# Three GpSimd drains inside the tile loop of a hard-max attention kernel, at tiles 28, 60 and 92

## The chip, the cores and the metric

The kernel runs on one core of a Trainium2 chip. The metric is the device time of one execution in microseconds (us). The kernel before takes 466.72 us (median of 3 runs, 466.47 to 467.32). All engine names are those of the profile: PE is TensorE, PEld its weight loads, DVE is VectorE, ACT is ScalarE, POOL (or Pool) is GpSimd, SP is SyncE.

## The reference

For each of 4 × 4096 queries, find the key with the largest dot product and return its value row:

```python
def reference(q, k, v):                                # each [4, 4096, 128] float32
    logits = np.matmul(q, k.transpose(0, 2, 1))
    best = np.argmax(logits, axis=-1)
    b_idx = np.arange(q.shape[0])[:, None]
    return v[b_idx, best, :].astype(np.float32)
```

## The kernel before

The 16384 queries are cut into T = 128 tiles of 128 queries. PE, ACT and DVE screen all keys of a tile in fp16. What DVE keeps is an index of a group of three keys per query (`cand`). Pool then gathers those three keys from memory (`kg`), and DVE computes their products with the query again (`prod`, then adds). Two tiles form a pair: it has two k gathers and one product. When a chunk of 4 or 8 tiles is through, DVE picks the winners (`win`), and Pool gathers their value rows (`vr`), which SP stores.

So for each tile Pool issues one k gather and one v gather. With the loads of later batches and some gathers for doubtful rows, these are 324 DMAs in the whole program, all started by instructions on Pool. The last of them is a scatter into the output.

The gathers are appended to queues. `near_q` holds k gathers and, after the last gather of each pair, a *mark*; `late_q` holds v gathers:

```python
    def gather(c, t0, n):                      # a pair: tiles t0, t0 + 1
        ...                                    # cut: cand on DVE
        kg = rp.tile([P, n, 3, P], FP16, tag=f"kg{n}", name=f"kg_{t0}", bufs=8)
        kg_t[t0] = kg
        for j in range(n):
            near_q.append(lambda j=j: nc.gpsimd.indirect_dma_start(
                out=kg[:, j].rearrange("p f d -> p (f d)"), out_offset=None, in_=k16[t0 // NQT],
                in_offset=IOA(ap=x[:, j:j + 1], axis=0)))
        mark = lambda: done.add(("kg", t0))
        marks.add(mark)
        near_q.append(mark)
        start(dots(c, t0, n), "dots", c)

    def dots(c, x, m):
        ...
        yield "until", lambda: ("kg", x) in done, 1 if x >= TAIL else 2     # TAIL = T - 24
        kg = kg_t.pop(x)
        prod = rp.tile([P, m, 3, P], FP16, tag=f"prod{m}", name=f"prod_{x}")
        nc.vector.tensor_tensor(out=prod, in0=kg, in1=natq[...], op=OP.mult)     # cut
```

At the end of each tile, `issue` decides which gathers go out:

```python
    def issue(it):
        n = 0
        clock[0] = it
        put_out(it)
        while near_q and (n < 1 + (it >= T - 28 and len(near_q) > 2) or near_q[0] in marks):
            g = near_q.pop(0)
            n += g not in marks
            g()
        if fast and it >= rest[0]:
            fast.pop(0)()
            rest[0] = it + 3
        take_late(2 if n == 0 and len(late_q) > 4 or it >= T - 24 and it % 2 == 0 else 1)
```

The loop calls it once per tile:

```python
    for it in range(T):
        ...                                    # cut: loads, transposes
        if it > 0:
            screen(it)                         # PE, ACT
        if it >= 1:
            fold(it - 1)                       # DVE: W
        ...
        step(it)                               # one DVE instruction of the products and picks
        if it >= 2:
            top(it - 2)                        # DVE: TOP
        if 3 <= it <= TAIL:
            gathers(it - 3)                    # DVE: cand, fills near_q
        if it >= TAIL:
            gathers(it - 2)
        step(it)
        issue(it)                              # Pool
```

The trace shows one more instruction of weight, which the code above doesn't contain: the program ends with a drain on Pool.

## Time and profile before

| | before |
|---|---|
| time, median of 3 runs | 466.72 us |
| span of the profiled run | 465.5 us |
| DVE busy | 417.8 us (90%) |
| Pool busy | 318.1 us (68%) |
| last product starts at | 425.92 us |
| from there to the end | 39.6 us |
| sequencer instruction before the last scatter (trace) | 2.41 us |
| final Pool drain (trace) | 10.49 us, 454.19 to 464.68 |

The first lines below are from the page of the profile before: the span, each engine's busy time, and the groups of the k gathers, the v gathers and the products. A group's line gives source line, engine, operation, what is written and read, and count; then busy time and mean nanoseconds of one; then idle time of the engine just before them and what ended most of it.

```profile
span 465.5 us, 6396 instructions
PE 380.2 (82%) x1834; PEld 168.3 (36%) x1834; DVE 417.8 (90%) x825; ACT 376.8 (81%) x437; POOL 318.1 (68%) x345
...
L250 POOL DMA_INDIRECT kg<-k,cand x128 | 127.4, 995 | 85.1 <-issue 26.6
...
L304 POOL DMA_INDIRECT vr<-in_v_dram,win x128 | 136.6, 1067 | 39.0 <-issue 37.5
...
L265 DVE TENSOR_TENSOR prod<-kg,natq 128x768 f16<-128x768 f16 x64 | 34.9, 546 | 3.9 <-DMA kg<-k,cand 3.9
```

DVE is the engine that sets the pace. Its products wait only 3.9 us for k gathers in the whole run.

The end is Pool's. This is Pool's timeline before, in its last 20 us (start, duration, engine, line, operation; in brackets the idle time before it and what ended that):

```profile
447.55 1.00 POOL L498 DMA_INDIRECT FV<-in_v_dram,xw_fe  x1 [2.19 <-DVE hi L573]
454.42 1.03 POOL L534 DMA_INDIRECT out_dram<-FV,rowk_e  x1 [5.87 <-issue]
```

After the scatter at 454.42 nothing more is busy, yet the run goes on for 10 us: that is the drain. Drains don't count as busy and don't stand in the timeline. The trace has them with start and end, and the times of drains here are read from it. The Trainium skill, "Perfetto Trace Analysis", section "Sequencer-only Instruction (DRAIN, etc)", draws a drain as an instruction of the sequencer alone; this trace agrees, since the final drain's record opens at 454.19 and the scatter executes on Pool from 454.42 to 455.45, inside it. A drain's own work is therefore counted below from the end of the last DMA: 464.68 − 455.45 = 9.23 us.

The other thing that stands out is two DMAs that start late for no reason that a wait shows. They are the ones with index 113 and 219 (counted from 0) in Pool's order; no semaphore instruction stands before them on Pool. (The scatters at 287 and 323 also start late, but the trace shows semaphore instructions just before them.) First the lines around index 113 (the load, which here follows a gather with 0.135 us of gap where other loads have none), then those around 219 (gap 0.79 where gathers have 0.30):

```profile
164.65 1.01 POOL L304 DMA_INDIRECT vr<-in_v_dram,win  x1 [0.30 <-issue]
165.79 0.59 POOL L67 DMA_DIRECT2D natq<-in_q_dram  x1
...
303.90 0.99 POOL L304 DMA_INDIRECT vr<-in_v_dram,win  x1 [0.30 <-issue]
305.68 0.95 POOL L250 DMA_INDIRECT kg<-k,cand  x1 [0.79 <-issue]
```

### The profile page before, as it was taken

The numbers are of one execution on the slowest core, as the hardware profiler recorded it, in microseconds if no ns is written. First come the engines' busy times: TensorE is split into PE (matmuls) and PEld (weight loads), VectorE is DVE, ScalarE is ACT, GpSimd is POOL, SyncE is SP. The second block draws the span as 40 slices with busy tenths as digits, with TensorE's granted clock in tenths as the row PEclk, the third lists the DMA queues.
The fourth block names the chain that finished last, engine by engine and source line by source line (L and its number), as shares of the span: only waits on it lengthen the run. The fifth ranks groups of instructions, "written<-read, shape, count | busy, mean of one in ns | idle before, by whom it ended". The sixth has DMA issues, their size and how long they took to land.

```text
span 465.5 us, 6396 instructions
## 1 busy us (share of the span) xinstructions
PE 380.2 (82%) x1834; PEld 168.3 (36%) x1834; DVE 417.8 (90%) x825; ACT 376.8 (81%) x437; POOL 318.1 (68%) x345
## 2 busy tenths in 40 slices
PE   8999999998999889999998889998998888850100
PEld 4444444443444344444443334443333333320000
DVE  2689999999999999999999999999998999998330
ACT  2999999999999989999997889999998888840000
POOL 8233557877677888776678876677777777767730
PEclk9999999999999999999999999999999999995555
DMA  7934576853325877943235653423432333322320
GB/s 130 227 66 96 107 103 97 139 120 85 80 76 135 148 140 128 121 126 81 79 98 137 129 116 94 100 80 87 110 101 79 86 86 99 87 71 68 94 74 4
DMA packets 43624, 47.54 MB, mean 102 GB/s; under 512 B 25000, under 2 KB 33451, under 8 KB 43584
## 3 DMA queue, kind: packets, MB, share of 16 engines
q0 software_dynamic: 18752, 30.97, 33.7%
q1 hardware_dynamic: 24832, 16.13, 13.1%
q8 instruction: 14, 0.23, 0.2%
q14 instruction: 26, 0.21, 0.2%
HBM read 39.59 MB, written 12.19 MB: 111 GB/s over the span
## 4 chain that ended last, share of the span: by engine, by line
DVE 31%; issue 23%; ACT 13%; PE 13%; DMA 9%; POOL 7%; POOLq 0%; DVEq 0%; ACTq 0%
DVE W L228 14%; ACT A L202 10%; PE psn L193 5%; DVE TOP L232 5%; PE psn L212 4%; DMA kg<-k,cand 4%; ACT E L215 4%; DMA vr<-in_v_dram,win 3%; DVE prod L265 3%; PE pd L193 3%; POOL kg L250 3%; POOL vr L304 2%; DVE D L274 2%; DVE p L269 2%; DMA natk<-in_k_dram 2%
## 5 line engine op out<-in xcount | busy, mean ns | idle before, releaser
L202 ACT ACTIVATE A<-pd 128x1024 f16<-128x1024 f32 x256 | 258.6, 1041 | 23.0 <-PE pd L193 22.7
L250 POOL DMA_INDIRECT kg<-k,cand x128 | 127.4, 995 | 85.1 <-issue 26.6
L228 DVE SCALAR_TENSOR_TENSOR W<-psn,E 128x1024 int16<-128x1024 f32 x128 | 166.0, 1297 | 7.0 <-ACT E L215 5.5
L193 PE MATMUL pd<-kT,qT 128*128 128x512 f16 x512 | 151.8, 378 | 15.7 <-ACT A L202 14.8
L193 PE MATMUL psn<-kT,qT 128*128 128x512 f16 x512 | 151.8, 378 | 15.3 <-ACT A L202 7.9
L304 POOL DMA_INDIRECT vr<-in_v_dram,win x128 | 136.6, 1067 | 39.0 <-issue 37.5
L193 PEld LDWEIGHTS <-qT 128*128 128x128 f16 x1024 | 98.4, 97 | 163.9 <-issue 76.0
L232 DVE MAX8 TOP<-W 128x8 f32<-128x1024 f32 x128 | 155.8, 1217 | 0.0
L212 PE MATMUL psn<-A,identh 128*128 128x512 f16 x512 | 152.1, 378 | 0.0
L215 ACT ACTIVATE E<-psn 128x1024 int16<-128x1024 f32 x128 | 132.2, 1033 | 5.0 <-PE psn L212 5.0
L212 PEld LDWEIGHTS <-identh 128*128 128x128 f16 x512 | 49.6, 97 | 60.8
L265 DVE TENSOR_TENSOR prod<-kg,natq 128x768 f16<-128x768 f16 x64 | 34.9, 546 | 3.9 <-DMA kg<-k,cand 3.9
L269 DVE TENSOR_TENSOR p<-prod 128x384 f16<-128x384 f16 x64 | 22.3, 349 | 0.1
L274 DVE TENSOR_REDUCE D<-p 128x6 f32<-128x192 f16 x64 | 21.5, 336 | 0.1
L173 ACT ACTIVATE kT<-uk 128x256 f16<-128x256 f32 x48 | 20.1, 419 | 0.9 <-PE uk L170 0.9
L64 POOL DMA_DIRECT2D natk<-in_k_dram x27 | 16.1, 599 | 0.9 <-POOLq L795 0.8
L67 POOL DMA_DIRECT2D natq<-in_q_dram x27 | 16.3, 605 | 0.2
L169 PE MATMUL uk<-identh,natk 128*128 128x128 f16 x96 | 15.8, 218 | 0.6 <-ACT A L202 0.6
L272 DVE TENSOR_TENSOR p<-p 128x192 f16<-128x192 f16 x64 | 15.7, 245 | 0.0
L464 PE MATMUL fp_e<-n_e,tri 128*128 128x1 f32 x2 | 0.6, 361 | 16.7 <-DVE n_e L462 16.7
L170 PEld LDWEIGHTS <-natk 128*128 128x128 f16 x96 | 9.3, 97 | 7.7 <-issue 5.3
L169 PEld LDWEIGHTS <-natk 128*128 128x128 f16 x96 | 9.3, 97 | 5.6
(147 smaller groups left out, 133.5 us busy)
## 6 DMA issues: line engine op xcount, KB each, us to landing
out_dram<-vr SPq DMA_DIRECT2D x32, 256.0 KB, 2.2
natq<-in_q_dram POOLq DMA_DIRECT2D x26, 128.0 KB, 3.2
k<-kd SPq DMA_DIRECT2D x8, 384.0 KB, 4.2
natk<-in_k_dram POOLq DMA_DIRECT2D x24, 128.0 KB, 3.9
kg<-k,cand POOLq DMA_INDIRECT x128, 2.8
vr<-in_v_dram,win POOLq DMA_INDIRECT x128, 2.8
natq<-in_q_dram POOLq DMA_DIRECT2D x1, 768.0 KB
natk<-in_k_dram POOLq DMA_DIRECT2D x1, 512.0 KB, 5.2
```

What stands on the lines that cost most here:

```text
L169: nc.tensor.matmul(out=o, lhsT=natk[b % 2][:, h, 4 * m + x, :], rhs=identh, start=True, stop=False)
L193: nc.tensor.matmul(out=ps[:, n * 512:(n + 1) * 512], lhsT=qT[b % 2][:, qt * P:(qt + 1) * P], rhs=kT[b % 2][:, u * 1024 + n * 512:u * 1024 ...
L202: nc.scalar.activation(out=A, in_=ps, func=AF.Abs)
L212: nc.tensor.matmul(out=ps[:, n * 512:(n + 1) * 512], lhsT=identh, rhs=A[:, n * 512:(n + 1) * 512], start=False, stop=True)
L215: nc.scalar.activation(out=E, in_=ps, func=AF.Relu, scale=QSCALE)
L228: nc.vector.scalar_tensor_tensor(out=W_t[t % NW].bitcast(I16)[:, 1::2], in0=ps, scalar=QSCALE, in1=E, op0=OP.mult, op1=OP.max)
L232: nc.vector.max(out=TOP[:, t, :], in_=W_t[t % NW].bitcast(FP32))
L250: near_q.append(lambda j=j: nc.gpsimd.indirect_dma_start(out=kg[:, j].rearrange("p f d -> p (f d)"), out_offset=None, in_=k16[t0 // NQT], ...
L265: nc.vector.tensor_tensor(out=prod, in0=kg, in1=natq[b % 2][:, x - b * NQT:x - b * NQT + m, :].unsqueeze(2).to_broadcast([P, m, 3, P]), op ...
L269: nc.vector.tensor_tensor(out=p1, in0=prod[:, :, :, 0:64], in1=prod[:, :, :, 64:128], op=OP.add)
L274: nc.vector.tensor_reduce(out=d[:, x - c0:x - c0 + m, 1:4], in_=p2, axis=AX_X, op=OP.add)
L304: late_q.append(lambda j=j: nc.gpsimd.indirect_dma_start(out=vr[:, j, :], out_offset=None, in_=v_flat, in_offset=IOA(ap=win[:, i + j:i + j ...
```

## The change

The intent, as the change reads: the final drain has something to clear up for the DMAs that Pool issued. If Pool clears part of it earlier, in the loop, where DVE sets the pace and Pool has spare time, then less is left for the end, where Pool is alone. To make room, the three tiles with a drain issue no gathers; the k gather is made up soon after, the v gathers within some tiles.

```diff
+DRAINS = (28, 60, 92)
 ...
     def issue(it):
         n = 0
         clock[0] = it
         put_out(it)
-        while near_q and (n < 1 + (it >= T - 28 and len(near_q) > 2) or near_q[0] in marks):
+        if it in DRAINS:
+            nc.gpsimd.drain()
+            owed[0] += 2
+            return
+        behind = len(near_q) > (2 if it >= T - 28 else 4)
+        while near_q and (n < 1 + behind or near_q[0] in marks):
             g = near_q.pop(0)
             n += g not in marks
             g()
         if fast and it >= rest[0]:
             fast.pop(0)()
             rest[0] = it + 3
-        take_late(2 if n == 0 and len(late_q) > 4 or it >= T - 24 and it % 2 == 0 else 1)
+        more = n == 0 and len(late_q) > 4 or it >= T - 24 and it % 2 == 0
+        if owed[0] and n < 2 and it % 3 == 0 and len(late_q) > 2:
+            owed[0] -= 1
+            more = True
+        take_late(2 if more else 1)
+
+    owed = [0]
```

## The prediction

> **What bounds the kernel now.** The page gives VectorE (DVE) 417.8 of 465.5 us busy (90%); in a table of 20 us windows it is full nearly throughout from 40 to 420 us. A tile costs it 3.0 to 3.3 us (distance of W folds in its timeline). GpSimd (Pool, 68%) runs beside it: in its timeline a k gather takes 0.98 us, a v gather 1.01, each after a 0.30 us issue gap, so 2.6 us per tile; with a load (0.60) 3.2. A gather lands 2.8 us after issue (DMA issues); usually 3 to 5 us pass between a pair's landing and its product on DVE, but at pairs 46 and 48 below 1 us, at pair 104 none. After 426 us comes a serial tail of 40 us, all Pool at its end: a sequencer instruction of 2.41 us (450.8), the last scatter (454.4) and the final Pool drain, 10.49 us (454.19 to 464.68). The scatter, at the usual 2.8 us, lands at 457.2; about 7.5 us of the drain is something else.
>
> **What the drain does.** I suppose it retires one record for each Pool DMA on a list. The Trainium skill, "DMA: Bandwidth & Descriptors", section "SWDGE vs HWDGE vs iDMA", says that GpSimd keeps its descriptors in rings in SBUF.[...] Of 324 Pool DMAs, two start late with no wait that explains it: index 113 (gap 0.135 instead of 0.00) and index 219 (0.79 instead of 0.30). I read these as the ring filling, being freed in bulk, cheaply, and filling again 106 later. Then some 112 records are left for the final drain: 7.5/112 = 0.067 us each (estimate).
>
> **The change.** Removed: 2.6 us of Pool work in each of tiles 28, 60, 92. Added: three drains behind about 64, 79 and 73 DMAs, by the same estimate 4.3, 5.3 and 4.9 us (about 2 us, the last landing, if retiring is cheap). Moved: the k gather is made up two tiles later; two v gathers come 5 and 8 tiles later, one more than skipped, so about three of the 11 v gathers after 424 us leave the tail. Left for the final drain: about 109 DMAs, no fewer than the 112 above. So I expect the final drain to stay at 10 us and the 2.41 us instruction too: the saving that the change seems made for does not come. Fewer v gathers in the tail save about 0.6 us.
>
> **On the critical path.** Replaying the timeline's Pool issues with these drains against the products' start times, DVE stalls little at 28, 1 to 2 us around tile 60, and most after 92, where Pool is busy without a break until 345 us and pair 104 has no slack: in all +6 us with 0.067 us per record, +1.5 us if a drain only waits for landings.
>
> **Prediction.** 470 us (+0.7%), 459.5 to 477 in 8 of 10. Faster by over 2%: 0.05; within 2%: 0.83; slower by over 2%: 0.12.
>
> **What would show it.** Right: three Pool drains of 4 to 6 us; a final drain of still 9 to 11 us; odd gaps at indices 113 and 219 gone; products waiting for k gathers after tiles 60 and 92; DVE busy time unchanged.
>
> **What would make it wrong.** If the list holds all 324 DMAs (0.023 to 0.028 us each), the loop's drains take about 2 us, fit into the freed tile, and the final drain falls to about 4 us and the 2.41 to about 0.8: then some 460 us. If drains only wait for landings, 467.5. If drains are dearer than estimated, over 476.

## More of the kernel before

The `yield "until"` line decides where the product stands in DVE's program: two tiles after the pair's mark, and one tile after it for pairs from tile 104 on. This is settled when the program is built.

The busy time of each engine in windows, in this order: window, length, PE, PEld, DVE, ACT, POOL, granted clock, DMA share, GB/s:

```profile
195.00:225.00 30.00, 28.72 (x142) 12.80 (x140) 30.00 (x51) 29.07 (x36) 20.81 (x22) 1.00 0.38 98
300.00:330.00 30.00, 27.94 (x126) 11.92 (x125) 30.00 (x54) 28.56 (x33) 22.80 (x23) 1.00 0.32 83
360.00:400.00 40.00, 33.06 (x137) 13.05 (x136) 39.56 (x95) 31.63 (x34) 29.79 (x31) 1.00 0.31 87
```

In two 30 us windows of the loop DVE has no idle time at all.

## The result, and the profile after

The changed kernel takes 482.78 us (median of 4 runs, 480.9 to 483.78) where the kernel before took 466.67 in the same rounds. The ratio is 1.0338, with a 95% interval of 1.0301 to 1.0375: slower by 3.4%.

| | before | after |
|---|---|---|
| span of the profiled run | 465.5 us | 480.2 us |
| DVE busy | 417.8 us | 418.8 us |
| products waiting for k gathers | 3.9 us | 17.3 us |
| last product starts at | 425.92 us | 440.11 us |
| from there to the end | 39.6 us | 40.1 us |
| sequencer instruction before the last scatter | 2.41 us | 2.31 us |
| final Pool drain | 10.49 us | 10.06 us |

The lines of the page after that answer to those of before:

```profile
span 480.2 us, 6397 instructions
PE 383.3 (80%) x1834; PEld 168.5 (35%) x1834; DVE 418.8 (87%) x825; ACT 377.6 (79%) x437; POOL 316.4 (66%) x345
...
L251 POOL DMA_INDIRECT kg<-k,cand x128 | 128.4, 1003 | 98.6 <-issue 38.1
...
L305 POOL DMA_INDIRECT vr<-in_v_dram,win x128 | 134.3, 1049 | 39.0 <-issue 36.9
...
L266 DVE TENSOR_TENSOR prod<-kg,natq 128x768 f16<-128x768 f16 x64 | 35.3, 551 | 17.5 <-DMA kg<-k,cand 17.3
```

Nothing got more work to do: DVE's busy time is the same within 1 us. Its products wait 13.4 us longer. The same windows as before:

```profile
195.00:225.00 30.00, 27.59 (x135) 12.29 (x134) 29.25 (x50) 27.99 (x35) 17.45 (x19) 1.00 0.33 81
300.00:330.00 30.00, 27.64 (x127) 11.79 (x126) 27.11 (x50) 28.17 (x32) 17.92 (x18) 1.00 0.27 70
360.00:400.00 40.00, 30.72 (x121) 11.77 (x120) 35.93 (x95) 28.42 (x31) 29.20 (x30) 0.96 0.29 84
```

In the first two windows, which hold a drain each, Pool is busy 3.4 and 4.9 us less than before and DVE now has 0.8 and 2.9 us of idle time. In the third there is no drain (the last drain ended at 312.41), and DVE still loses 3.6 us against before. So a second cause seems to act late in the loop. The waits of DVE for k gathers split between the two stretches. These are the lines of the waits of after, first in the window from 95 to 366 us, then in that from 366 to 441 us, each with total, count and longest:

```profile
DVE prod L266 <- DMA kg<-k,cand: 8.6, 12, 2.5
...
DVE prod L266 <- DMA kg<-k,cand: 8.8, 4, 3.7
```

In the same two windows of before the totals were 2.9 and 1.0 us. (The windows are the same times, not the same tiles, in the two kernels.)

Pool's timeline of after shows what a drain costs. The three stretches below are around tiles 28, 60 and 92:

```profile
100.87 1.22 POOL L305 DMA_INDIRECT vr<-in_v_dram,win  x1 [0.30 <-issue]
108.18 1.07 POOL L251 DMA_INDIRECT kg<-k,cand  x1 [6.08 <-issue]
...
202.09 1.01 POOL L305 DMA_INDIRECT vr<-in_v_dram,win  x1 [0.30 <-issue]
210.47 0.94 POOL L251 DMA_INDIRECT kg<-k,cand  x1 [7.37 <-DVE p L273]
...
305.39 1.01 POOL L305 DMA_INDIRECT vr<-in_v_dram,win  x1 [0.30 <-issue]
313.21 0.98 POOL L251 DMA_INDIRECT kg<-k,cand  x1 [6.82 <-issue]
```

The bracket's second part is to be read with care: the view puts the 7.37 us down to an instruction of DVE, because that was the last event before the gather that the view knows. The drain's own record in the trace covers the gap. Pool stands still for 6.08, 7.37 and 6.82 us. And the end of after looks as the end of before did:

```profile
462.12 0.99 POOL L499 DMA_INDIRECT FV<-in_v_dram,xw_fe  x1 [5.25 <-DVE rowk_e L533]
469.53 1.03 POOL L535 DMA_INDIRECT out_dram<-FV,rowk_e  x1 [6.42 <-issue]
```

The drains as the trace has them, with the DMAs issued since the last drain:

| drain of after | drain's record | last DMA ends | drain's end minus last DMA's end | DMAs since the last drain | per DMA |
|---|---|---|---|---|---|
| tile 28 | 96.79 to 107.39 | 102.09 | 5.30 us | 64 | 0.083 us |
| tile 60 | 198.47 to 209.69 | 203.09 | 6.60 us | 80 | 0.082 us |
| tile 92 | 302.57 to 312.41 | 306.39 | 6.02 us | 73 | 0.082 us |
| final | 469.30 to 479.36 | 470.56 | 8.80 us | 107 | 0.082 us |
| final, before | 454.19 to 464.68 | 455.45 | 9.23 us | 324 | 0.028 us |

Four drains of the same kernel agree on 0.0825 us per DMA. The final drain of before doesn't fit, unless its list had only 9.23 / 0.0825 = 112 entries. The late starts of before at index 113 and 219 are gone in after.

### The profile page after: what moved, and what is told of

The parts are those of the page before. It is cut to its first block, busy times and chain, and to the rows that moved or that the text cites. A ratio compares the mean times of both kernels' runs of the same rounds, so it can differ in the third digit from the quotient of the medians.

```text
span 480.2 us, 6397 instructions
## 1 busy us (share of the span) xinstructions
PE 383.3 (80%) x1834; PEld 168.5 (35%) x1834; DVE 418.8 (87%) x825; ACT 377.6 (79%) x437; POOL 316.4 (66%) x345
## 4 chain that ended last, share of the span: by engine, by line
DVE 28%; issue 25%; POOL 13%; DMA 12%; PE 11%; ACT 7%; POOLq 1%; DVEq 0%; ACTq 0%
DVE W L229 14%; POOL vr L305 6%; DMA kg<-k,cand 6%; POOL kg L251 5%; ACT A L203 4%; PE psn L194 4%; DVE TOP L233 4%; PE pd L194 4%; PE psn L213 3%; DVE prod L266 3%; DMA FK<-in_k_dram,gb_e 3%; ACT E L216 2%; DVE D L275 2%; DVE p L270 2%; DMA vr<-in_v_dram,win 2%
## 5 line engine op out<-in xcount | busy, mean ns | idle before, releaser
L305 POOL DMA_INDIRECT vr<-in_v_dram,win x128 | 134.3, 1049 | 39.0 <-issue 36.9
L266 DVE TENSOR_TENSOR prod<-kg,natq 128x768 f16<-128x768 f16 x64 | 35.3, 551 | 17.5 <-DMA kg<-k,cand 17.3
L171 PEld LDWEIGHTS <-natk 128*128 128x128 f16 x96 | 9.3, 97 | 7.5 <-issue 4.8
L245 DVE TENSOR_SCALAR cand<-TOP 128x2 uint32<-128x2 uint32 x64 | 11.4, 179 | 0.4
```

The lines of the kernel that those rows point to most:

```text
L266: nc.vector.tensor_tensor(out=prod, in0=kg, in1=natq[b % 2][:, x - b * NQT:x - b * NQT + m, :].unsqueeze(2).to_broadcast([P, m, 3, P]), op ...
L305: late_q.append(lambda j=j: nc.gpsimd.indirect_dma_start(out=vr[:, j, :], out_offset=None, in_=v_flat, in_offset=IOA(ap=win[:, i + j:i + j ...
```

## The experiments

Two theories were needed from the start, because two stretches of the loop lose time.

- **Theory R (records).** Each Pool DMA leaves one record on a list. A drain retires them one by one, at 0.0825 us, and Pool issues nothing meanwhile. When the list is full (113 entries), it is emptied in bulk and cheaply, but for about 7 entries, so that it is full again 106 DMAs later. This is why before leaves 112 for the end, and why three drains in the loop, the last one 107 DMAs before the end, save nothing there.
- **Theory S (snapshot).** `behind`, computed once per tile, issues both gathers of a pair in one tile from tile 100 on. The pair's mark is set a tile sooner, its product stands a tile sooner in DVE's program, and DVE waits for the gather to land.
- **Rivals.** Against R: a drain's time is the landing of what is in flight, or the final drain's size belongs to the program's end and not to a list. Against S: the drains explain all of the loss, or Pool's changed order (v gathers and loads) does, not the product's place.

Eighteen runs were made on several chips. On three occasions the chip was disturbed for the whole job: the kernel before itself took about 512 us there, at a granted clock of about 0.92 instead of 0.95, with DVE waiting more for PE (its W folds 15 to 35 us in these runs, 1.5 us in before). Such waits hide waits for gathers: the snapshot alone shows 1.8 us of them on such a chip and 7.6 us on an undisturbed one. Times of those runs decide nothing here that is smaller than about 2%; their traces still show the drains. Most of those kernels were run again on an undisturbed chip.

### Drains without the snapshot

The changed kernel, with the test made again before each gather from tile 100 on:

```diff
-        while near_q and (n < 1 + behind or near_q[0] in marks):
+        while near_q and (n < 1 + (behind and (it < T - 28 or len(near_q) > 2)) or near_q[0] in marks):
```

First run (disturbed chip):

> The changed kernel, but from tile 100 on the test for a second gather is made anew before each gather, as in the kernel before. Theory A (the change loses twice: the three drains hold Pool back 6.1, 7.4 and 6.8 us, and separately the test that is made only once per tile issues both gathers of a pair in one tile from tile 100 on, so that their product comes one tile sooner and waits for the landing): about 474 us, the products of pairs 114 to 126 no longer 9 to 14 us later than before but about 7. Rival B (the drains' lag alone loses everything): about 482 us, as the changed kernel.

It took 533.12 us against 512.51, ratio 1.0375 (1.0281 to 1.047). Run again:

> The same kernel as drains_live once more, because the first time even the kernel before took 512 us on that chip. As ratios to before: theory A 1.016 (474 of 466.7), rival B 1.034.

On the undisturbed chip it took 476.86 us against 466.93 (ratio 1.0216, 1.018 to 1.0252): +9.9 us. Products wait 13.0 us for k gathers. The drains last as in after (5.30, 6.59, 6.02 and 8.80 us beyond the last DMA). So the drains alone cost about 10 us, and they don't explain all of the 16.

### The snapshot without drains

The changed kernel with `DRAINS = ()`. As `owed` stays 0, what is left of the change is `behind`:

```diff
-DRAINS = (28, 60, 92)
+DRAINS = ()
```

First run (disturbed chip):

> The changed kernel with an empty list of drains: what is left is the test that is made once per tile. Theory A: about 473 us, with 5 to 8 us of products waiting for k gathers after tile 100. Rival B: 467 us, the same as before. Late starts at Pool DMA 113 and 219 back again in both, and a final drain of about 10.5 us.

It took 522.59 us against 512.51, ratio 1.0154 (1.0068 to 1.024). Run again:

> The same kernel as snapshot_only once more. Ratio to before: theory A 1.012 to 1.016, rival B 1.00.

On the undisturbed chip it took 472.94 us against 466.93 (ratio 1.0137, 1.0098 to 1.0175): +6.0 us, without any drain in the loop. The two parts, +9.9 and +6.0, add up to the change's +16.1. The lag of the W fold of a tile (DVE's first instruction for it) behind the same fold of before, worked out from the traces, shows where each part is lost:

| lag in us at tile | 40 | 62 | 72 | 99 | 114 | 127 |
|---|---|---|---|---|---|---|
| after | +1.4 | +2.4 | +4.1 | +7.1 | +10.7 | +14.2 |
| drains, test made again | +1.2 | +1.4 | +3.9 | +6.9 | +7.8 | +10.1 |
| snapshot, no drains | +0.2 | −0.4 | −0.4 | −0.4 | +0.6 | +4.0 |

The totals add up, but the stages don't: at tile 114 the parts give 7.8 + 0.6 = 8.4 us where the change lags 10.7. So the two interact, and that their totals meet so closely may be chance. The profiled runs of before and of the snapshot are only 4.9 us apart: 3.8 us come before the last product (with 3.7 us more of waits for gathers) and 1.1 us after it.

The drains' loss comes in steps after tiles 28, 60 and 92. The snapshot's comes after tile 106. The last 2.4 us of the drains' row come at tiles 122 to 124, where a scatter of the flagged rows starts 2.9 us late; no run tested why.

### The skipped tiles without the drain

The change with the test made again and the skipped gathers made up, but no drain instruction:

```diff
         if it in DRAINS:
-            nc.gpsimd.drain()
             owed[0] += 2
             return
```

> The three tiles without gathers and the gathers made up later, with the test made anew from tile 100 on, but without the drain instructions. If the drains themselves cost what drains_live loses, this runs within 0.3% of before; if moving the gathers costs it, this is as slow as drains_live. Late starts at Pool DMAs 113 and 219 are back and the final drain is 10.5 us.

It took 466.42 us (ratio 0.9981, 0.9944 to 1.0018), and its products wait 3.0 us. Skipping and making up costs nothing. The drains' 9.9 us are the drains' time on Pool.

### The product held back again

Theory S says that the snapshot hurts through the product's place. So the snapshot without drains was given products two tiles after the mark to the end:

```diff
-        yield "until", lambda: ("kg", x) in done, 1 if x >= TAIL else 2
+        yield "until", lambda: ("kg", x) in done, 2
```

First run (disturbed chip):

> snapshot_only with the products of tiles from 104 on scheduled two tiles after their gathers instead of one. If snapshot_only loses its 6 us because the test that is made once per tile issues both gathers of a pair in one tile and so brings the product forward by a tile, to before the landing: the waits of products for gathers in the late loop fall from 7.6 to under 3 us and the time comes back to 466 to 468 us. If it loses them because the gathers crowd out other Pool work: stays at 473.

It took 521.01 us, ratio 1.0263 (1.0204 to 1.0322), worse than theory S says. But on that chip products hardly waited for gathers with or without the edit (0.9 us in this run, 1.8 us in the snapshot alone), so the run couldn't show what it was made for. Run again:

> The kernel before with the once-per-tile test and no drain (470.4 us of span on an undisturbed chip, 7.6 us of products waiting for k gathers, ratio 1.0137), and in addition the product of a pair comes two tiles after its last gather was issued, to the end (there it was one tile from pair 100 on). The last chip that ran this was disturbed and masked the waits. Theory: the 6 us are products that come a tile sooner and wait for their landing. Then the waits for k gathers fall to under 4 us and the last product starts before 428 us; the tail may grow by up to 3 us because the pairs' products come a tile later. Time 466 to 470. Rival: the 6 us are Pool's changed order (v gathers or loads late), not the product's place: then the waits stay near 7 us or move to another tile, and the time stays at 472 or more.

On an undisturbed chip it took 465.66 us against 466.89 (ratio 0.9988, 0.996 to 1.0015). The whole loss of the snapshot is gone, a little below the lower end of what theory S expected. These are the lines for waits of products in the whole run, of the snapshot and then of the snapshot with the product held back:

```profile
DVE prod L266 <- DMA kg<-k,cand: 7.6, 5, 2.4
```

```profile
DVE prod L266 <- DMA kg<-k,cand: 2.1, 3, 0.9
```

The time from the landing of a pair's last gather to its product, worked out from the traces (us; about 0 means that the product started as soon as the gather had landed; where the trace has no landing, it is put 2.8 us after issue, the median):

| pair | 114 | 116 | 118 | 120 | 122 | 124 | 126 |
|---|---|---|---|---|---|---|---|
| before | 1.30 | 1.24 | 0.04 | 1.80 | 4.12 | 0.89 | 0.03 |
| snapshot | 0.0 | 0.1 | 0.1 | 0.0 | 0.2 | 1.2 | 0.1 |
| snapshot, product held back | 1.6 | 1.3 | 0.1 | 2.5 | 5.1 | 2.2 | 0.0 |

In the snapshot, six of these seven products start within 0.2 us of the landing. Before three of them (116, 118 and 126) DVE stood idle, for 1.9, 1.2 and 1.7 us; before the others it was busy until then. It looks like a loop that feeds itself, since the next `cand` on DVE, and with it the next gather, comes after the product; this was not tested. Pool's order of DMAs is the same in both kernels for the first 284 of the 324, up to about 392 us, and differs from that of before from index 236 on. Within this common stretch the fold of tile 114 already lies 3.1 us apart (lag +0.6 in the snapshot, −2.5 with the product held back). So the rival (Pool's order) falls there. After it the order follows the products' place, and the two can't be told apart. One correction to the text: it says that the one-tile place begins with pair 100; in the code it begins with 104.

Could holding back be a gain of its own, which would hide some cost of the snapshot? A control, the kernel before with the same one-line edit:

> The control for the once-per-tile test with products held two tiles (465.66 us, ratio 0.9988): the kernel before with nothing but products held two tiles to the end. Theory: the once-per-tile test costs nothing of its own, its 6 us are the products that come a tile sooner. Then this control is as fast as that run within 2 us: 464 to 468.5 us, and the waits for k gathers are under 4 us. Rival: the later product by itself is a gain that hides a cost of the test: then this control is at 463 us or less.

It fell on a disturbed chip: 511.05 us against 512.79, ratio 0.9976 (0.9906 to 1.0046). It shows no gain larger than about 1%. The profile of before gives a closer estimate. The edit touches only pairs from 104 on, and there the products of before wait 2.8 us (pair 104 1.8, pair 126 1.0). That is about what holding them back can take away, if a microsecond of wait costs a microsecond, as it did in the loop of the snapshot (3.7 and 3.8 us). The cause is shown but for a remainder of this size: some 3 of the 6.0 us are surely the product's place.

The same edit in the whole changed kernel:

> The changed kernel whole (three drains, test once per tile), with products held two tiles to the end. Theory: this undoes the once-per-tile test's part alone and leaves the drains' part, so it is as the drains with the live test (476.9 us, ratio 1.0216): 474 to 479 us, waits for k gathers 10 to 14 us. Rival: the parts overlap, the drains make Pool late enough that a later product gains little: 480 us or more.

This too fell on the disturbed chip: 533.51 us, ratio 1.0426 (1.0319 to 1.0534). The drains with the live test had 1.0375 (1.0281 to 1.047) on such a chip, in another job. The intervals overlap, and the numbers in us were meant for an undisturbed chip. It decides nothing.

### One drain only, at tile 28

If theory R holds, the place of a drain counts. A drain at index 64 moves the next filling to 64 + 113 = 177 and the one after to 283, which leaves 324 − 283 + 7 = 48 entries for the end:

```diff
-DRAINS = (28, 60, 92)
+DRAINS = (28,)
```

(with the test made again before each gather). Two runs on the disturbed chip:

> Only the drain at tile 28, with the test made anew from tile 100 on. Theory C (Pool's list of DMAs is emptied in bulk, except for some 7, whenever it has 113; a drain walks what is left at 0.0825 us each): the late starts move to Pool DMAs about 177 and 283, the final drain finds about 48 records and takes 5 to 5.5 us instead of 10.5, the sequencer instruction before it about 1.1 us instead of 2.4; in all 461 to 463 us. Rival D (nothing but a drain empties the list): the final drain walks 260 DMAs and takes over 20 us, or the 10.5 us are constant and stay.

> The same kernel as drain28_only once more, on a chip where before takes 467 us: the loop loses 1.2 us to the drain at tile 28 (as far as drains_live_2 lost by tile 46), the final drain takes 5.25 instead of 10.49 and the sequencer instruction 1.14 instead of 2.41: about 461.5 us, ratio 0.988.

They took 515.55 us (ratio 1.0014, 0.9929 to 1.0098) and 511.81 us (1.0057, 0.9993 to 1.0122). The traces show the drain at tile 28 at 5.30 us, a late start at index 177 and a final drain of 5.25 us, 3.99 beyond the last DMA: 48 entries at 0.083 us. But no gain in time could be seen. The third run was on an undisturbed chip:

> Only one drain, at tile 28, with the live test; run twice on a disturbed chip (ratios 1.001 and 1.006). Its records: 64 retired at tile 28 in 5.3 us, 48 left for the final drain, 5.25 us instead of 10.49, and the sequencer instruction at 1.1 instead of 2.4 us. Theory: pair 28's slack hides the held-up Pool, so the loop loses at most 2 us and the end saves 6.5: 460.5 to 463.5 us, ratio 0.986 to 0.993. Rival: the loop pays for each drain what the end saves (the disturbed runs): 465 to 468.

It took 460.76 us against 466.89 (ratio 0.9889, 0.9859 to 0.992): 6.1 us faster than before. Its last product starts at 425.26, no later than before's, and from there to the end it takes 33.1 us instead of 39.6. The end of Pool's timeline, to set beside that of before (6.87 us from one start to the next there):

```profile
446.78 0.99 POOL L499 DMA_INDIRECT FV<-in_v_dram,xw_fe  x1 [2.17 <-DVE hi L574]
452.53 1.03 POOL L535 DMA_INDIRECT out_dram<-FV,rowk_e  x1 [4.76 <-SPq L577]
```

From the one DMA to the next it is 5.75 us here, because the sequencer instruction between them fell from 2.41 to 1.14 us. So the change's intent works with the first of its three drains alone: pair 28 has slack (4.7 us from landing to product in before) that hides most of Pool's standstill, and 48 entries instead of 112 are left. Part of that is luck: the fold of tile 40 comes 1.1 us later than in before, and it is regained between the folds of tiles 109 and 110, where before waits 1.8 us for pair 104 and this kernel doesn't. No run tested why.

### One drain at tile 50, just after a filling

At tile 50 the list should have been emptied in bulk four DMAs ago. Theory R expects a short drain there; the rival that a drain pays for all 117 DMAs since the start expects 9.7 us. For the end theory R expects 324 − 117 − 106 = 101 entries:

```diff
-DRAINS = (28, 60, 92)
+DRAINS = (50,)
```

(here too with the test made again before each gather)

First run (disturbed chip):

> One drain, at tile 50, just after the ring has been emptied in bulk at Pool DMA 113; 117 DMAs have been issued by then. Theory C (a drain pays for what is on the list): 11 records, the drain ends 1.0 us after the last DMA before it, holds Pool back 1.8 us and costs the loop nothing; the next bulk emptying comes at DMA 230, the final drain walks 101 records, 9.6 us in all; 466 us. Rival E (a drain pays for every DMA since the last drain): it ends 9.7 us after the last DMA before it, and the loop loses 5 us.

It took 518.56 us (ratio 1.0208, 1.0118 to 1.0299). The drain lasted 3.55 us beyond the last DMA. That is neither number. The final drain was 8.32 us beyond the last DMA, 101 entries at 0.0824, as R said, and the next late start was at index 230, which is 117 + 113. Run again:

> One drain, at tile 50, just after the list should have been emptied by filling up. On the disturbed chip it lasted 3.55 us beyond the last DMA's end and 101 records were left for the final drain. Theory: that time is the landing of the load that was issued last, not records: the drain ends within 0.3 us of that landing again, Pool is held up about 4 us, the final drain is 9.3 to 9.8 us. DVE loses 2 to 5 us: 468 to 471 us, ratio 1.003 to 1.010.

On an undisturbed chip it took 474.0 us against 466.89 (ratio 1.0151, 1.0128 to 1.0175), so worse than the 468 to 471 expected. The drain's end is 3.60 us behind the last DMA's end, the final drain again has 8.32 us. Pool's timeline around the drain:

```profile
169.75 0.60 POOL L65 DMA_DIRECT2D natk<-in_k_dram  x1
174.53 0.56 POOL L65 DMA_DIRECT2D natk<-in_k_dram  x1 [4.17 <-PE pd L194]
```

The load before the drain was issued at 169.75; the profile's DMA issues give such loads 3.9 us from issue to landing in before, and 4.4 in after, so it lands at about 173.65 to 174.15 (estimate from those medians), and the drain ends at 173.95. Its own landing is not recorded in the trace; its last packet there ends at 173.13, 0.82 us before the drain does (0.80 us in the first run). By theory R the drain had 11 entries, which is 1.0 us. So something beyond its entries holds this drain for 2.6 us. The landing of what was issued last fits, but no run varied it, so it is not shown. The rival of 117 entries falls. What the expectation got wrong is DVE's loss: the fold's lag is already +5.2 at tile 62, and +7.7 at tile 127, for a standstill of 4.2 us. The delayed load and gathers are both in that stretch (products wait 10.3 us in the whole run); which of them weighs more was not tested. This kernel pays for a drain and gets nothing at the end.

### Fewer records at the end, without any drain

If filling up empties the list cheaply, then no drain is needed: it is enough to move the fillings so that the last one comes shortly before the end. A needless load of 27 pieces per partition at the start takes the place of several ordinary DMAs on the list:

```diff
     load_q(0, 8, NQT)
+    scratch = bp.tile([P, 27, 16], FP16, name="scratch", tag="scratch")
+    nc.gpsimd.dma_start(out=scratch, in_=q[0].rearrange("(p t) d -> p t d", p=P)[:, 0:27, 0:16])
```

Its result is never read. First run (disturbed chip):

> The kernel before with no drain, but one needless GpSimd load at the start, of 27 pieces of 16 numbers per partition[...]. Theory C: the ring fills sooner, at the DMAs of about index 90, 196 and 302; the final drain then finds about 30 records and takes about 4 us instead of 10.5, the sequencer instruction before it about 0.8; in all about 459 us. Rival D: final drain unchanged at 10.5 us or longer, 467 us.

It took 503.38 us against 512.51 (ratio 0.9826, 0.9735 to 0.9916). Run again:

> The same kernel as phase27 once more: final drain 3.8 us, the sequencer instruction 0.8 us; 458 to 459 us where before is 466.7, ratio 0.982.

On the undisturbed chip it took 458.8 us against 466.93 (ratio 0.9825, 0.9793 to 0.9857). The final drain is 3.80 us, 2.53 beyond the last DMA: 30 entries at 0.084, as theory R said. The first late start moved to index 90, the sequencer instruction fell to 0.78 us. So the needless load takes as much of the list as 24 others (113 − 89): what fills up is not counted in whole DMAs, as the "113 entries" of theory R would have it. This is the strongest evidence for R against the rivals, because the last DMAs and the program's end are the same as before.

The same edit with 15 pieces (`[P, 15, 16]` and `0:15`) should leave some 19 entries (325 − 313 + 7). First run (disturbed chip):

> As phase27 with 15 pieces instead of 27: the last bulk emptying comes at about DMA 313 in the tail, the final drain finds about 19 records and ends 1.65 us after the last DMA, 2.9 us in all, the sequencer instruction about 0.6; the emptying itself costs about 0.5 us in the tail; 458 to 459 us, no clear difference from phase27.

It took 509.97 us (ratio 0.9949, 0.9818 to 1.0081), with a final drain of 3.27 us. Run again:

> The kernel before with a needless load of 15 pieces at the start instead of 27. On the disturbed chip the final drain was 3.27 us with about 18 records left, where 27 pieces left 30 and 3.80 us. Theory: the scatter's landing is a floor under the final drain, so it is no shorter than 3.2 us; the time is as with 27 pieces within 1 us, 457.5 to 459.5, ratio about 0.982. Rival without a floor: 457 or less.

It took 457.33 us against 466.89 (ratio 0.9801, 0.978 to 0.9822): the fastest kernel here, about 2% faster than before, and 5% below the 482.78 us that the change took in its own rounds. The final drain is 3.27 us again, 2.01 beyond the last DMA, more than 19 entries explain (1.6 us). The scatter's landing doesn't account for it: in the five traces that have it (after is one), it comes 1.2 us after the scatter's end, and this drain lasts 0.8 us longer. The time is a hair below the range that the theory gave. So the floor is not shown, and what the remaining 0.4 us are stays open.

```profile
445.64 0.99 POOL L500 DMA_INDIRECT FV<-in_v_dram,xw_fe  x1 [2.08 <-DVE hi L575]
451.54 1.03 POOL L536 DMA_INDIRECT out_dram<-FV,rowk_e  x1 [4.91 <-SPq L578]
```

All drains together, those with a direct count of DMAs since the last drain first, then those whose count rests on theory R:

| entries | 64 | 73 | 80 | 107 | 30 | 48 | 101 | 112 |
|---|---|---|---|---|---|---|---|---|
| drain's end minus last DMA's end, us | 5.30 | 6.02 | 6.60 | 8.80 | 2.53 | 3.99 | 8.32 | 9.23 |

A straight line, about 0.09 + 0.0814 us per entry, goes through all eight within 0.03 us. That the list is the cost, and not the drain itself, shows in a second way: on Pool another drain follows the final one with no DMA between them, and it takes 0.11 us in before.

## Why the prediction was wrong

**Right: the final drain stays.** Predicted 9 to 11 us; it is 10.06, with 107 entries where 109 were predicted. The 10 us test the count, not the cost of one entry: any cost fitted to the 10.49 us of before gives about 10 us for nearly as many entries. The instruction of 2.41 us stays too (2.31). The saving that the change seems made for doesn't come, because the list was already being emptied: before leaves 112 for the end, the change 107.

**Right: the list, and where DVE would stall.** The two late starts vanish, DVE's busy time is unchanged, and products wait after tiles 60 and 92. At tile 28 little is lost (1.2 us with the drains alone). "Most after 92" was not right: the lag grows by 3.3 us between tiles 56 and 72 (from +0.6 to +3.9), and by 3.0 after 92.

**Wrong in size: "7.5/112 = 0.067 us each".** The subtraction took the walk to begin only when the scatter has landed, at 457.2. The line through the eight drains begins at the last DMA's end instead (455.45 here), so the term is 9.23 / 112 = 0.0825 us. To it comes about 0.8 us from the drain's end until the next gather starts, which the prediction left out. Pool is held back 6.1, 7.4 and 6.8 us where 4.3, 5.3 and 4.9 were predicted. The drains cost 9.9 us where the prediction had +6 for its figure of 0.067 (its 470 us lies between that and its other case, a drain that only waits for landings). Of the 9.9 us, 2.4 are the unexplained step at tiles 122 to 124. The 0.6 us that it expected to win in the tail didn't come (40.1 us instead of 39.6); with the drains alone the tail does get shorter, to 38.6 us. The prediction even named this: "If drains are dearer than estimated, over 476". The drains alone give 476.86.

**Wrong in kind: the snapshot was not seen.** The failed step is "Moved". The prediction has no term for `behind`. The sentence "Moved: the k gather is made up two tiles later" stands for everything that it says of the order of k gathers. The diff's change of *when* a condition is evaluated, from before each gather to once per tile, costs 6.0 us without any drain, and with the product held back the time is that of before again (465.66 us).

The sum: 466.7 + 9.9 + 6.0 = 482.6, measured 482.78. The two single parts are measured, the second's cause is shown but for the remainder named above.

**Still open.** Why the two drains at 60 and 92 cost DVE 3 us each and the one at 28 only 1 was argued from the slack between landing and product, not tested one by one. The fillings of the list are inferred: their late starts are seen at index 113 and 219 in before, 177, 230, 90, and 101 and 207 in the others, but they last 0.1 to 2.1 us, and at some predicted places (196 and 302 with 27 pieces, 283 with a drain at 28, 313 with 15 pieces) no unexplained one shows. The counts at the end fit all the same.

## What to carry to other kernels

Before moving a cost out of a kernel's end, find out how much of it is really there: a final drain that fits 112 of 324 DMAs says that the list is emptied on the way, and then shifting the phase of that emptying is worth more than doing the work by hand in a loop that has no room. A drain holds back everything behind it on its engine (6.1 to 7.4 us in after), so put one only where the next consumer has more slack than the drain's length. And read a diff for when a condition is evaluated: a test hoisted out of a loop moved the consumers in another engine's program, and cost more than a third of the loss.

## What the Trainium skill lacked or had wrong

- "DMA: Bandwidth & Descriptors", section "SWDGE vs HWDGE vs iDMA", says that GpSimd appends descriptors to rings in a carved-out part of SBUF. The late starts fit a ring of limited length. The page doesn't say that a drain on GpSimd pays for each DMA still on it: 0.0825 us each, from 30 to 112 entries.
- The same section doesn't say what happens when the ring is full. Here 113 DMAs seem to fill it; all but about 7 seem then to be retired, in 0.1 to 2.1 us, far less than the 8.7 us (106 × 0.0825) that a drain takes for as many.
- No page has the cost of Pool's sequencer instruction ahead of the last scatter (INC_SWDGE_SEM in the trace): 2.41 us with about 112 entries on the list, 1.14 with 48, 0.78 with 30, 0.56 with 19, which is 0.02 us for each.
- "VectorE: DVE Perf Modes", section "The DRAIN you can't avoid", says of the drains that come with every program's start and end that they are about 12 ns, on all five engines. It names them as the runtime's own. The trace of before has 17 drains, all with lines of the program: the 13 of the other engines take 7 to 80 ns, but the four on Pool 168 ns at the start and 10.49 us, 109 and 46 ns at the end. If they are the drains that the page means, its figure doesn't hold for Pool; if they are not, no page has their cost.
- No page says whether a drain on Pool waits for the landing of a DMA. With a load issued last and some 11 entries on the list, it ended 3.6 us beyond that load's end, where 11 entries give 1.0 us.
